# Hybrid decoder trunk on one core: zero products at the start, a reordered opening, and gate and keys of the second unit computed tile by tile with the first unit

## The chip, the cores and the metric

The kernel runs on one core of a Trainium2 chip. The metric is the device time of one execution in microseconds (us), lower is better; where several runs are compared, their median is used.

The engines are called by their names or by the short forms of the profile: TensorE (PE, its weight loads PEld), VectorE (DVE), ScalarE (ACT), GpSimd (POOL), and SyncE (SP), whose queue issues the kernel's DMAs.

## The reference, cut to what matters

One layer of a decoder trunk, 2048 tokens of width 1024, in float32:

```python
mod = (silu(c) @ w_ada + b_ada)                      # 6 x 1024: sh1, sc1, g1, sh2, sc2, g2
h = rms_norm(x) * (1.0 + sc1) + sh1
x = x + g1 * token_mixer(h, ...)                     # one input projection, three kinds of heads, one output projection
h = rms_norm(x) * (1.0 + sc2) + sh2
x = x + g2 * conv_ffn(h, ...)                        # up-projection, causal depthwise conv, silu gate, down-projection
return rms_norm(x) * final_gain
```

The token mixer has three groups of heads: HGRN2 heads (forget `f = lb + (1-lb)*sigmoid(z)`, key `1 - f` scaled by the bound, queries through silu, values, an output gate), GLA heads (a gate of rank 16: `logsigmoid(alow @ w_gla_up + b) / 16`, keys, queries, values, output gate) and retention heads (rotary, fixed decay). Each is a causal recurrence that is computed in chunks.

## The kernel before, in words

**Layout.** Tokens go in four blocks of 512 (`b`). Features lie on the partitions: the normalised input of a block is eight tiles `h[k]` of 128 features by 512 tokens. Every float32 product is made of three products of a split: each operand has a high part (rounded to the type that TensorE multiplies fast) and a low part (the rest), and `hi*hi + hi*lo + lo*hi` is accumulated (`split3`, lines 246 to 248). ScalarE casts the high part, VectorE subtracts to get the low part.

**Conditioning.** `mod` has 48 columns of 128. Column `m` is a dot product on VectorE of one weight tile (`wada[m]`, 512 KB) with `c_act = silu(c)`, which is held on all partitions (`ada`, line 197). Columns 0 to 7 are the shifts, 8 to 15 the scales of the first norm, one for each `h[k]`.

**Units.** The mixer of a block is a list of units: `ORDER = h0, g, h1, h2, h3, r0, r1`. `unit_h` makes the products for two HGRN2 heads (forget `f`, queries `q`, values and gates `vg`), `unit_g` those of the GLA heads (low-rank gate `al` and keys `ak`, then queries `aq`, then values and gates), `unit_r` those of retention. Behind its projections, each unit hands the recurrence to a chain (`gated`: dot products `dt`, seven levels `lv` of the chunk tree, transposes, state update, output, head norm `post`, transposed result `oT`). TensorE's order is the order of the program. A planner (`Clock`) decides where the chain's steps stand in it: each projection matmul that is emitted advances its clock (`adv`, 0.227 us for 512 columns), each chain step has a due time, and chains run one after another. `clock.until` empties due steps without products between them; one such place is ahead of the second half of the output projection of a block, in the next block behind its first unit. VectorE, ScalarE and SP are ordered by a scheduler with priorities (`tc.high_priority(offset)` puts instructions ahead by so many), except inside `startup`.

**The opening** (`startup`, lines 376 to 484) is the first block's norm together with the first unit's products, in an order written out by hand for VectorE, ScalarE and SP. The eight tiles of x are loaded, squared on ScalarE and summed on VectorE (line 346); four matmuls with a column of ones sum over partitions (`ssn`, line 418); a reciprocal square root is iterated on VectorE (`newton`); a matmul broadcasts it (`bcn`, line 426). Then for each tile k: `scaled` (line 352, VectorE), `high` (line 356, ScalarE), `low` (line 359, VectorE), and the products of the first unit that this tile allows, as far as the weights' parts are there (`put`, `flush`). The tuple `plan` says for each k which conditioning tiles are loaded, which dot products stand ahead of the scaling (`first`), which between high and low part (`then`), and which weight gets its low part. Weight tiles pass through two raw buffers (`wraw`), conditioning tiles through a ring of eight (`a4k`), on which SP waits in order.

**Around it.** `norm1_stat` and `norm1_h` make the norm of the next block during the current one; the broadcast follows the sums by 4.5 us of the planner's clock (`rstd`, line 330). `tok_evac` and `tok_evac4` read values and gates out of PSUM. The channel mixer behind the four blocks (from about 1,280 us on) is not touched.

Of the kernel before, what the change touches and what calls it, by code (L numbers as in the profile page):

```python
# [9 lines left out]
F32 = mybir.dt.float32  # L10
# [7 lines left out]
P = 128  # L18
# [29 lines left out]
CHAIN = 400  # L48

# [51 lines left out]
def trunk(ctx, tc, xT, vecs, cvec, cst, rope, msk, wada, win, walow, wgla, wout, wup, wdown, out):  # L101
# [39 lines left out]
    nc.sync.dma_start(vec[:], vecs)  # L141
# [7 lines left out]
    nc.sync.dma_start(c_all[:], cst)  # L149
# [13 lines left out]
    lg = vec[:, V_LB:V_LB + 4]  # L163
    e = small("lbe", 4)
    V.tensor_tensor(e[:], lg, lg, op=ALU.subtract)
    S.activation(e[:], e[:], AF.Exp)
    r = small("lbr", 4)
    V.reciprocal(r[:], e[:])
    V.tensor_tensor(e[:], e[:], r[:], op=ALU.mult)
    V.tensor_tensor(lb[:], e[:], e[:], op=ALU.subtract)  # L170
    V.tensor_scalar(oml[:], lb[:], -1.0, 1.0, op0=ALU.mult, op1=ALU.add)
# [4 lines left out]
    nc.sync.dma_start(craw[:], cvec.to_broadcast([P, D]))  # L176
    S.activation(c_act[:], craw[:], AF.Sigmoid)
    V.tensor_tensor(c_act[:], c_act[:], craw[:], op=ALU.mult)
# [3 lines left out]
    for g in (1, 4):  # L182
        V.tensor_scalar(bada1[:, 8 * g:8 * g + 8], bada1[:, 8 * g:8 * g + 8], 1.0, None, op0=ALU.add)

# [133 lines left out]
    def rstd(acc, name, bc, then, bank=None):  # L318
# [3 lines left out]
        def first():  # L322
# [7 lines left out]
            clock.at(4.5, lambda: second(r))  # L330
# [45 lines left out]
    def startup():  # L376
# [3 lines left out]
        for k in range(KD):  # L380
            x.append(x_tile(f"x0_{k}", k))
            nc.sync.dma_start(x[k], xT[0, :, k, :])
        raws = {}

        def weight(name, i, extra=False):
            raw = pw.tile([P, 1024], F32, tag="wraw", name="r" + name, bufs=NRAW)
            nc.sync.dma_start(raw[:], win[i])
            if extra:
                t = [pa.tile([P, 1024], F32R, tag="a4k", name=n + name) for n in "hl"]
            else:  # L390
                t = [pw.tile([P, 1024], F32R, tag="w" + n, name=n[0] + name) for n in ("hi", "lo")]
            W[name] = [*t, raw, i]

        def cast(name):
            S.copy(W[name][0][:], W[name][2][:])

        def low_part(name):
            hi, lo, raw, i = W[name]
            V.tensor_tensor(lo[:], raw[:], hi[:], op=ALU.subtract)

# [6 lines left out]
        load(8, 0)  # L407
        weight("f", 1)
        load(9)
        weight("q", 0)  # L410
        load(1, 2)
        acc = new_acc("n1_0")
        for k in range(KD):
            sumsq(acc, x[k], k, "n1_0_")
        cond(8)
        ps = late_ps("ssn1_0")
        for c in range(NCH):
            T.matmul(ps[:, c:c + 1], acc[:, c * P:(c + 1) * P], ones, start=True, stop=True)
        ms, r = small("msn1_0", NCH), small("rsn1_0", NCH)
        V.tensor_scalar(ms[:], ps[:, 0:NCH], 1.0 / D, EPS, op0=ALU.mult, op1=ALU.add)  # L420
        newton(ms, r, NCH)
        cast("f")
# [5 lines left out]
        cond(9)  # L428
        S.copy(bc[:], ps[:])
        cast("q")  # L430
# [3 lines left out]
        def put(kind, k, w):  # L434

            two = (0, 1) if w == 0 else (0,)
            if kind in "fq":
                sl = slice(k * P, (k + 1) * P)
                for p in two:
                    T.matmul((pf if kind == "f" else pq)[:], W[kind][w][:, sl], h[k][:, p, :],  # L440
                             start=k == 0 and w == 0 and p == 0, stop=k == KD - 1 and w == 1, skip_group_check=True)
            else:
                sl = slice((k % 4) * 256, (k % 4 + 1) * 256)
                for c in range(NCH):
                    for p in two:
                        T.matmul(pv[c // 2][:, (c % 2) * 256:(c % 2) * 256 + 256], h[k][:, p, c * P:(c + 1) * P],
                                 W[f"v{k // 4}"][w][:, sl], start=k == 0 and w == 0 and p == 0 and c % 2 == 0,
                                 stop=k == KD - 1 and w == 1 and c % 2 == 1, skip_group_check=True)

        def flush():  # L450
            for q in list(pending):
                if (q[0] if q[0] in "fq" else f"v{q[1] // 4}") in parts[q[2]]:
                    pending.remove(q)
                    put(*q)
# [4 lines left out]
        parts = {"f", "q"}, set()  # L459
        for k, (ld, first, then, wl) in enumerate(plan):  # L460
            if k == 0:
                weight("v0", 2)
            if k == 3:
                weight("v1", 3, True)
            load(*ld)
# [4 lines left out]
            if k in (1, 4):  # L470
                name = "v0" if k == 1 else "v1"
                cast(name)
                parts[0].add(name)
# [3 lines left out]
            if wl:  # L477
                low_part(wl)
                parts[1].add(wl)
            pending += [(kind, k, w) for w in (0, 1) for kind in "fqv"]  # L480
            flush()
        assert not pending
        ready["hfh0_0"], ready["hqh0_0"], ready["vgh0_0"] = pf, pq, pv
        return W

    def norm1_stat(b):
# [6 lines left out]
        clock.at(22.0, rstd(acc, f"n1_{b}", bc1[b][:], lambda: done.add(("n1", b))))  # L493
# [966 lines left out]
```

## Time and profile before

| | |
|---|---|
| median of 3 runs | 2587.08 us (2585.16 to 2595.53) |
| profiled execution | 2597.18 us, span 2595.4 us |
| TensorE busy | 2520.8 us, 97% of the span |
| VectorE busy | 1986.9 us, 77% |
| ScalarE busy | 1115.7 us, 43% |
| mean granted clock of TensorE | 0.992 |
| first product of the opening | 23.03 us |
| end of the opening's products | 58.42 us |

How to read it: the profile is of one execution, and its own time lies above the median of the runs. TensorE is nearly always busy, so time is to be had only where it waits or where its clock is lowered; the opening holds the longest such stretch. In the rows below, the first two numbers of a row of the timeline are start and duration in us, and the bracket at the end tells how long the engine had been idle and what ended that. A row that stands for several instructions gives their count behind an x.

### The profile page before, as it was taken

Reading aid. Unit: us, or ns where it says so; the run is one execution under the profiler, and the core shown is the slowest. Engines: PE = TensorE matmul, PEld = TensorE weight load, DVE = VectorE, ACT = ScalarE, POOL = GpSimd, SP = SyncE. Lnnn points to the kernel's source line nnn. Section 1 sums busy time; section 2 is a strip of 40 time slices with the busy share of each in tenths; the row PEclk is TensorE's granted clock in tenths of the full one; section 3 lists DMA queues with packets and bytes.
Section 4 is the critical chain, followed back from the end, with each engine's and each line's share of the span. In section 5 each row is a group of like instructions: output and inputs, shape, how many; then the busy total and the mean of one; then the engine's idle time right before and its main releaser. Section 6 shows DMA issues by size and latency. Waiting matters only on the chain.

```text
span 2595.4 us, 37081 instructions
## 1 busy us (share of the span) xinstructions
PE 2520.8 (97%) x13132; PEld 2137.3 (82%) x13132; DVE 1986.9 (77%) x3627; ACT 1115.7 (43%) x1897; POOL 144.2 (6%) x246
## 2 busy tenths in 40 slices
PE   5999999999999999999999999999999999999997
PEld 4798878998889888998778888878878888888886
DVE  8778986868768786887688888876677777788565
ACT  3333434433333234333355445455444544555442
POOL 1000010000000000000010000000000010010000
PEclk9999999999999999999999999999999999999998
DMA  8543656765687846877665444487665544447663
GB/s 304 192 156 131 213 215 232 276 211 181 220 294 273 291 166 221 298 278 254 221 221 170 151 154 147 157 277 237 204 224 165 158 136 146 150 134 271 200 189 111
DMA packets 231753, 533.88 MB, mean 206 GB/s; under 512 B 25072, under 2 KB 26128, under 8 KB 231568
## 3 DMA queue, kind: packets, MB, share of 16 engines
q1 hardware_dynamic: 231568, 531.52, 60.3%
q8 instruction: 103, 1.69, 0.3%
q14 instruction: 82, 0.67, 0.1%
HBM read 397.72 MB, written 133.69 MB: 205 GB/s over the span
## 4 chain that ended last, share of the span: by engine, by line
PE 88%; DVE 7%; DMA 3%; issue 1%; ACT 1%; SPq 0%; DVEq 0%; ACTq 0%
PE X L246 6%; PE X L247 6%; PE X L248 6%; PE lvh L622 3%; PE Z L247 3%; PE Z L248 3%; PE Z L246 3%; PE dX L246 3%; PE dX L248 3%; PE dX L247 3%; PE dY L246 2%; PE dY L248 2%; PE dY L247 2%; PE psqkvgr L248 2%; PE psqkvgr L246 2%; PE psqkvgr L247 2%
## 5 line engine op out<-in xcount | busy, mean ns | idle before, releaser
L246 PE MATMUL X<-B,A 128*128 128x512 f32 x572 | 224.5, 393 | 1.3 <-ACT u L1245 1.3
L247 PE MATMUL X<-B,A 128*128 128x512 f32 x572 | 223.9, 391 | 0.2 <-DMA B<-made 0.2
L248 PE MATMUL X<-B,A 128*128 128x512 f32 x572 | 223.9, 391 | 0.0
L973 DVE TENSOR_TENSOR dA<-rd,dA 128x512 fp32r<-128x512 f32 x154 | 106.3, 690 | 100.9 <-ACT dA L972 100.7
L972 ACT CAST dA<-rd 128x512 fp32r<-128x512 f32 x154 | 95.4, 619 | 159.5 <-PE dY L248 53.2
L973 DVE TENSOR_TENSOR A<-s,A 128x512 fp32r<-128x512 f32 x176 | 120.7, 687 | 40.9 <-ACT A L972 40.8
L246 PE MATMUL psvgh<-hvgh,ha 128*128 128x256 f32 x480 | 140.1, 292 | 0.0
L248 PE MATMUL dX<-dB,dA 128*128 128x512 f32 x352 | 139.1, 395 | 0.0
L247 PE MATMUL dX<-dB,dA 128*128 128x512 f32 x352 | 139.1, 395 | 0.0
L246 PE MATMUL dX<-dB,dA 128*128 128x512 f32 x352 | 139.1, 395 | 0.0
L248 PE MATMUL psvgh<-hvgh,ha 128*128 128x256 f32 x480 | 135.9, 283 | 0.0
L247 PE MATMUL psvgh<-lvgh,ha 128*128 128x256 f32 x480 | 135.9, 283 | 0.0
L972 ACT CAST A<-s 128x512 fp32r<-128x512 f32 x176 | 108.4, 617 | 61.8 <-PE Z L248 46.8
L246 PEld LDWEIGHTS X<-B,A 128*128 128x128 f32 x572 | 107.5, 188 | 25.1 <-ACT u L1245 2.2
L247 PEld LDWEIGHTS X<-B,A 128*128 128x128 f32 x572 | 107.5, 188 | 24.0 <-DMA B<-made 0.9
L248 PEld LDWEIGHTS X<-B,A 128*128 128x128 f32 x572 | 107.5, 188 | 23.2
L246 PE MATMUL Z<-B,A 128*128 128x512 f32 x308 | 122.0, 396 | 2.2 <-ACT B L972 1.7
L247 PE MATMUL Z<-B,A 128*128 128x512 f32 x308 | 121.7, 395 | 0.3 <-DVE B L973 0.3
L248 PE MATMUL Z<-B,A 128*128 128x512 f32 x308 | 121.7, 395 | 0.0
L622 PEld LDWEIGHTS lvh<-qbh,kh 128*128 128x128 f32 x896 | 115.2, 191 | 7.7 <-issue 1.4
L622 PE MATMUL lvh<-qbh,kh 128*128 128x128 f32 x896 | 120.1, 277 | 0.3 <-DVE kh L632 0.3
L973 DVE TENSOR_TENSOR A<-r,A 128x512 fp32r<-128x512 f32 x130 | 89.5, 688 | 30.3 <-ACT A L972 30.3
(440 smaller groups left out, 7127.7 us busy)
## 6 DMA issues: line engine op xcount, KB each, us to landing
gs<-yv SPq DMA_DIRECT2D x154, 256.0 KB, 2.8
rb<-gs SPq DMA_DIRECT2D x154, 256.0 KB, 4.0
r<-wup SPq DMA_DIRECT2D x141, 256.0 KB, 3.4
s<-sumsu SPq DMA_DIRECT2D x132, 256.0 KB, 3.0
wada<-wada SPq DMA_DIRECT2D x48, 512.0 KB, 4.8
rd<-sumsd SPq DMA_DIRECT2D x88, 256.0 KB, 3.8
rd<-wdown SPq DMA_DIRECT2D x66, 256.0 KB, 3.5
x<-xT SPq DMA_DIRECT2D x64, 256.0 KB, 5.1
```

What stands on the lines that cost most here:

```text
L246: T.matmul(ps, lhs[0], rhs[0], start=first, stop=False, skip_group_check=more)
L247: T.matmul(ps, lhs[0], rhs[1], start=False, stop=False, skip_group_check=more)
L248: T.matmul(ps, lhs[1], rhs[0], start=False, stop=last, skip_group_check=more)
L622: T.matmul(ps[:, c * P:(c + 1) * P].rearrange("p (h n s) -> p h n s", h=2, s=s), kq[:, c * P:(c + 1) * P], rhs, start=True, stop=True)
L972: S.copy(hi, src)
L973: V.tensor_tensor(lo, src, hi, op=ALU.subtract)
```

## The change

- **Zero products.** A tile of zeros is set on VectorE, and eight 128x512 float32 matmuls of it go ahead of all other products on TensorE, into a bank that is used later.
- **Opening, loads.** x comes in four DMAs of two tiles instead of eight of one; the vector c comes between the second and third of them, the constants (`cst`) behind the first conditioning tile. The gate's weights are loaded in the opening. Value weights go through other buffers, so that their load does not wait for a raw buffer.
- **Opening, conditioning.** The sigmoid of c stands behind the fifth square on ScalarE; the product for `c_act` and the additions to the bias stand behind the sums of squares on VectorE. Squares go to a ring of six buffers instead of two. In `plan`, the dot products stand ahead of the scaling for every tile but the first, and the first has two between high and low part (9 and 1).
- **Gate and keys of the GLA unit** (`l`: 16 matmuls, `k`: 24) are done in the opening tile by tile, in the two banks of the chain's levels. In block 0 `unit_g` takes them as ready, and the planner's clock is not advanced for them. `flush` emits products whose weights were there before the current tile ahead of those whose weights just came.
- **Read-out of values and gates** (`tok_evac`, `tok_evac4`) at a raised priority (`EVAC = 300`).
- **Forget factor and key of the HGRN2 units** on ScalarE instead of VectorE.
- **Broadcast of the next block's first norm** due 10.0 us of the planner's clock behind the sums, instead of 4.5.

```diff
@@ startup: head
+        still = tmp("still")
+        V.memset(still[:], 0.0)
+        nc.sync.dma_start(vec[:], vecs)
+        lower_bounds()
+        idle = acc_ps("idle")
+        for _ in range(8):
+            T.matmul(idle[:], still[:, 0:P], still[:], start=True, stop=True)
+        for k in range(0, KD, 2):
+            if k == 4:
+                nc.sync.dma_start(craw[:], cvec.to_broadcast([P, D]))
+            x += [x_tile(f"x0_{k}", k), x_tile(f"x0_{k}", k + 1)]
+            nc.sync.dma_start(pair[0][:].rearrange("p (a n) -> p a n", a=2), xT[0, :, k:k + 2, :])
...
+        acc = new_acc("n1_0")
+        S.activation(acc[:], x[0], AF.Square)
+        for k in range(1, KD):
+            t = tmp(f"sqn1_0_{k}")
+            S.activation(t[:], x[k], AF.Square)
+            V.tensor_tensor(acc[:], acc[:], t[:], op=ALU.add)
+            if k == 4:
+                S.activation(c_act[:], craw[:], AF.Sigmoid)
+        load(8)
+        nc.sync.dma_start(c_all[:], cst)
+        load(0)
         weight("f", 1)
+        al = gla_load()
         load(9)
         weight("q", 0)
-        load(1, 2)
+        load(1)
+        weight("v0", 2, "b")
+        load(10, 2)
+        V.tensor_tensor(c_act[:], c_act[:], craw[:], op=ALU.mult)
+        for g in (1, 4):
+            V.tensor_scalar(bada1[:, 8 * g:8 * g + 8], bada1[:, 8 * g:8 * g + 8], 1.0, None, op0=ALU.add)
@@ startup: order by tile (ld, first, then, wl)
-        plan = [((10,), (), (1,), "f"), ((3, 11), (), (2,), "q"), ((4,), (10,), (3,), "v0"),
-                ((12, 5), (11,), (4,), None), ((13, 6), (12,), (5,), "v1"), ((14, 7), (13,), (6,), None),
-                ((15,), (14,), (7,), None), ((), (15,), (), None)]
+        plan = [((11, 3, 12), (), (9, 1), "f"), ((4, 13), (), (), "q"), ((5,), (10, 2), (), "v0"),
+                ((14, 6), (11, 3), (), None), ((15, 7), (12, 4), (), "v1"), ((), (13, 5), (), "k"),
+                ((), (14, 6), (), None), ((), (15, 7), (), None)]
...
+            pending += [(kind, k, w, p) for w, p, kinds in ((0, 0, "fqvlk"), (0, 1, "fqvlk"), (1, 0, "fqvk"))
+                        for kind in kinds]
@@ tok_evac (tok_evac4 alike)
-            S.copy(v[:, c2, :], p3[:, :, 0:P])
-            S.activation(sg[:, c2, :], p3[:, :, P:256], AF.Sigmoid)
-            V.tensor_tensor(sg[:, c2, :], sg[:, c2, :], p3[:, :, P:256], op=ALU.mult)
+            with tc.high_priority(offset=EVAC):
+                S.copy(v[:, c2, :], p3[:, :, 0:P])
+                S.activation(sg[:, c2, :], p3[:, :, P:256], AF.Sigmoid)
+                V.tensor_tensor(sg[:, c2, :], sg[:, c2, :], p3[:, :, P:256], op=ALU.mult)
@@ unit_h
-        V.tensor_scalar(f[:], sf[:], oml[:, u:u + 1], lb[:, u:u + 1], op0=ALU.mult, op1=ALU.add)
-        V.tensor_scalar(kq[:], sn[:], oml[:, u:u + 1], None, op0=ALU.mult)
+        S.activation(f[:], sf[:], AF.Identity, bias=lb[:, u:u + 1], scale=oml[:, u:u + 1])
+        S.activation(kq[:], sn[:], AF.Copy, scale=oml[:, u:u + 1])
@@ norm1_stat, unit_g
-        clock.at(22.0, rstd(acc, f"n1_{b}", bc1[b][:], lambda: done.add(("n1", b))))
+        clock.at(22.0, rstd(acc, f"n1_{b}", bc1[b][:], lambda: done.add(("n1", b)), gap=10.0))
...
-        ps = acc_ps("al" + nm)
-        for k in range(KD):
+        ps = ready.pop("al" + nm, None) or acc_ps("al" + nm)
+        for k in range(KD if b else 0):
```

More of the change, by code (lines that the diff above doesn't have):

```diff
@@ L48 @@
 CHAIN = 400
+EVAC = 300
 M512, M256, MF = 0.227, 0.12, 0.224
@@ L315, in tf512, with rstd @@
         return pss
-    def rstd(acc, name, bc, then, bank=None):
+    def rstd(acc, name, bc, then, bank=None, gap=4.5):
         bank = bank or late_ps
@@ L329, in first @@
                 newton(x, r, NCH)
-            clock.at(4.5, lambda: second(r))
+            clock.at(gap, lambda: second(r))
         def second(r):
@@ L395, in cast @@
             S.copy(W[name][0][:], W[name][2][:])
+            parts[0].add(name)
         def low_part(name):
@@ L399, in low_part @@
             V.tensor_tensor(lo[:], raw[:], hi[:], op=ALU.subtract)
+            parts[1].add(name)
         def cond(m):
@@ L427, in startup, with put @@
         cond(0)
[L428 removed]
+        cast("f")
         S.copy(bc[:], ps[:])
[L430 removed]
         pf, pq = acc_ps("pshfh0_0"), acc_ps("pshqh0_0")
         pv = [acc_ps(f"psvgh0_0_{j}") for j in range(NCH // 2)]
[L434 to L437 removed]
+        pl, pk = lev_ps("alg0"), lev_ps("psakg0")
+        whole = {"f": pf, "q": pq, "k": pk}
+        def put(kind, k, w, p):
+            first, last = k == 0 and w == 0 and p == 0, k == KD - 1 and (w == 1 or kind == "l" and p == 1)
+            if kind == "l":
+                T.matmul(pl[0:32, :], alow[:, k, :], h[k][:, p, :], start=first, stop=last, skip_group_check=True)
+            elif kind in whole:
                 sl = slice(k * P, (k + 1) * P)
[L439 to L441 removed]
+                T.matmul(whole[kind][:], W[kind][w][:, sl], h[k][:, p, :], start=first, stop=last,
+                         skip_group_check=True)
             else:
@@ L469, in startup @@
             high(x[k], k, "0_")
[L470 to L473, printed above, removed]
+            for at, name in ((0, "q"), (1, "v0"), (3, "v1"), (4, "k")):
+                if k == at:
+                    cast(name)
             for m in then:
```

102 lines of the change are left out of this document (49 added, 53 removed).

## Prediction

> **What bounds the kernel now.** I read the page first, then busy time by stage, then the order of instructions of the first 71 us, then every wait of TensorE behind it.
>
> ```profile
> span 2595.4 us, 37081 instructions
> PE 2520.8 (97%) x13132; PEld 2137.3 (82%) x13132; DVE 1986.9 (77%) x3627; ACT 1115.7 (43%) x1897; POOL 144.2 (6%) x246
> PE 88%; DVE 7%; DMA 3%; issue 1%; ACT 1%; SPq 0%; DVEq 0%; ACTq 0%
> ```
>
> TensorE is busy for 2520.8 of 2595.4 us, so an edit that leaves its products alone can win at most the 74.6 us between, plus what a lowered clock costs. The profiled execution took 2597.2 us, its span and 1.8 around it; the median of the runs is 10.1 lower, so I sum against 2597.2 and take the difference off the median, 2587.1.
>
> ```profile
> 4.00:6.00 2.00, 0.00 (x0) 0.00 (x0) 0.69 (x2) 0.59 (x1) 1.89 (x5) 1.00 0.91 199
> 8.00:10.00 2.00, 0.00 (x0) 0.00 (x0) 1.77 (x3) 1.84 (x4) 1.31 (x3) 1.00 1.03 385
> 30.00:52.00 22.00, 18.97 (x104) 15.95 (x104) 21.58 (x33) 4.55 (x6) 2.87 (x3) 1.00 1.01 388
> 331.00:341.60 10.60, 10.60 (x40) 8.72 (x41) 7.53 (x17) 3.19 (x4) 3.12 (x5) 0.71 0.56 198
> 743.90:754.60 10.70, 10.62 (x42) 8.82 (x43) 5.62 (x12) 0.76 (x4) 0.00 (x0) 0.71 0.55 193
> ```
>
> Columns are PE, PEld, DVE, ACT, POOL, granted clock, DMA share, GB/s. From 30 to 52 us VectorE is busy for 21.58 of 22.00: the tile-by-tile opening is bound by VectorE, not by products. In the last two stretches the clock is 0.71; both follow a stall of TensorE (below). The lost 0.29 of 10.6 us is 3.1 us each.
>
> ```profile
> 3.31 1.28 ACT L177 ACT_TABLE_LOAD   x1
> 6.65 1.06 ACT L177 ACTIVATE c_act<-craw 128x1024 f32<-128x1024 f32 x1 [2.06 <-DMA craw<-cvec]
> 7.74 1.23 DVE L178 TENSOR_TENSOR c_act<-c_act,craw 128x1024 f32<-128x1024 f32 x1 [3.02 <-ACT c_act L177]
> 9.09 5.47 DVE L346 TENSOR_TENSOR san<-san,sqn 128x512 f32<-128x512 f32 x7
> 13.00 0.63 ACT L345 ACTIVATE sqn<-x 128x512 f32<-128x512 f32 x1 [0.16 <-DVE san L346]
> 16.52 0.16 DVE L420 TENSOR_SCALAR msn<-ssn 128x4 f32<-128x4 f32 x1 [0.75 <-PE ssn L418]
> 18.71 2.08 PE L426 MATMUL bcn<-c_all,rsn 128*128 128x128 f32 x8 [2.23 <-DVE rsn L158]
> 21.44 0.75 DVE L352 SCALAR_TENSOR_TENSOR x<-x,mod,bc 128x512 f32<-128x512 f32 x1 [0.38 <-ACT bc L429]
> 22.11 1.28 DVE L197 CUSTOM_DVE_ANT_0 wada<-wada,c_act,vec 128x1024 f32<-128x1024 f32 x1
> 23.31 0.75 DVE L359 SCALAR_TENSOR_TENSOR ha<-x,mod,ha 128x512 fp32r<-128x512 f32 x1
> 23.98 1.22 DVE L399 TENSOR_TENSOR lf<-rf,hf 128x1024 fp32r<-128x1024 f32 x1
> 25.11 0.75 DVE L352 SCALAR_TENSOR_TENSOR x<-x,mod,bc 128x512 f32<-128x512 f32 x1
> 30.15 1.28 DVE L197 CUSTOM_DVE_ANT_0 wada<-wada,c_act,vec 128x1024 f32<-128x1024 f32 x1 [1.08 <-DMA wada<-wada]
> 53.23 0.75 DVE L352 SCALAR_TENSOR_TENSOR x<-x,mod,bc 128x512 f32<-128x512 f32 x1
> 54.02 0.72 ACT L356 ACTIVATE ha<-x,mod 128x512 fp32r<-128x512 f32 x1 [3.14 <-DVE x L352]
> 54.78 0.75 DVE L359 SCALAR_TENSOR_TENSOR ha<-x,mod,ha 128x512 fp32r<-128x512 f32 x1 [0.79 <-ACT ha L356]
> 57.80 0.62 PE L446 MATMUL psvgh<-lv,ha 128*128 128x256 f32 x4
> 59.85 0.42 PE L743 MATMUL alg<-ha,alow 128*32 128x512 f32 x1 [1.42 <-ACT snh L707]
> 68.81 0.39 PE L248 MATMUL psakg<-ha,lakg 128*128 128x512 f32 x1
> 70.76 0.48 PE L246 MATMUL psaqg<-ha,haqg 128*128 128x512 f32 x1
> ```
>
> The sums of squares end at 14.56 (9.09 + 5.47). The first tile is scaled at 21.44, the last low half ends at 55.53, the products of the opening at 58.42. Gate and keys run from 59.85 to 69.04, and the gate unit's queries begin at 70.76, behind 1.7 us of the first unit's chain. From start to start VectorE spends 0.67 on a scaling or a low half, 1.20 on a conditioning dot product and 1.13 on a weight's low half.
>
> **The opening, step by step.** The gate (16 matmuls) and the keys (24) leave the stretch behind the opening: 59.85 to 69.04, 9.2 us, and the 1.43 us wait ahead of it. I take 69.0 as the time at which the old kernel would have begun the queries without that piece of chain, and ask when the new one does.
>
> *Sums of squares.* The x loads come in pairs with the vector c between the second and third. Two pairs of 0.52 MB at 385 GB/s take 2.7 us, c at the 199 GB/s of the stretch in which it was loading 2.6, the third pair 1.4; from 2.5 us, with 0.8 to landing, tile 4 is there at about 10.0 (8.5 to 11). ScalarE then runs in its fixed order: square 0.63, table load 1.28 and sigmoid 1.06, which now stand between square 4 and square 5, three squares at 0.66, and VectorE's last add 0.75: 15.7 against 14.56. The old kernel had that table load done while it waited for data. A reader of the Trainium skill, page "ScalarE: Activation LUTs", section "What ACT_TABLE_LOAD costs", finds about 2.66 us for a switch with its drain, and the advice to batch calls by set, which speaks against putting a sigmoid among the squares; the row shows 1.28, by the page the sum would be 1.4 us worse, and I keep the row.
>
> *To the first scaling.* The product for c_act (1.23) and the two small bias adds (some 0.4) now stand behind the sums, then one conditioning (1.28); the sums' matmuls are hidden under these. From there the old rows repeat: 16.52 to 18.71 for the square root, 18.71 to 21.44 for the broadcast. 15.7 + 1.2 + 0.4 + 1.3 + 2.2 + 2.7 = 23.5 against 21.44.
>
> *Scaling to last low half.* This took 34.1 us (21.44 to 55.53). Added: the conditioning of m = 9, which was ahead of it, 1.2; the keys' low half, 1.1. In the old plan a conditioning stood between scaling and low half of every tile but the last and covered ScalarE's high half; in the new one only tile 0 has that. The last tile's rows show the bare cost: 53.23 to 54.78 is 1.55 instead of 0.67, so 0.88 for each of six more tiles, 5.3. Gone: the wait of 1.08 at 30.15, since the value weights no longer queue on SP behind the forget weights' buffer. 34.1 + 1.2 + 1.1 + 5.3 - 1.1 = 40.6, so 64.1.
>
> *Tail and next stage.* Behind the last low half come 2.6 us of products against 2.9 before, so 67.0 with the same hand-over; the queries' first matmul then waits for a bank that ScalarE has to read out, and for its own weights' split, like the gate did: 1.4. That is 68.4 against 69.0: **a gain of 0.6 us**. Bounds: minus 3 (ScalarE reads out values before the forget bank) to plus 6 (tile 4 two us earlier, no table load, half of the six gaps filled). TensorE itself is no bound: the new products add five 128x512 matmuls a tile, 40 x 0.23 = 9.2 us, to a stretch in which VectorE needs 40.6.
>
> *Zero products.* They run while nothing else is there to do, so they cost nothing; only if cold and some 2 us each could they last to about 18 us, and c_act and conditioning cover that. Do they warm the clock for what follows? The 0.71 at 331 us stands behind waits of 2.63 and 1.57 us only (below). Between the zero products and the sums lie several us, and 4 us more before the broadcast, so I count no gain; if the clock held, the broadcast's 2.08 would halve, plus 1.0. The Trainium skill, "TensorE: Matmul & The Clock Gate", part 1, says that an idle window of about 3.4 us closes the gate again; by that rule the zero products warm nothing that the sum needs, and the trace agrees, with even shorter waits.
>
> **Behind the opening.**
>
> ```profile
> 114.08 0.50 PE L248 MATMUL pshfh<-ha,lhfh 128*128 128x512 f32 x1 [1.17 <-DVE lhfh L230]
> 132.27 1.12 PE L559 MATMUL oTh<-c_all,oh 128*128 128x128 f32 x4 [2.44 <-DVE oh L553]
> 328.93 0.50 PE L246 MATMUL pshfh<-ha,hhfh 128*128 128x512 f32 x1 [2.63 <-ACT ha L356]
> 330.99 0.79 PE L247 MATMUL pshfh<-ha,hhfh 128*128 128x512 f32 x1 [1.57 <-DVE ha L359]
> 399.42 0.79 PE L335 MATMUL bcn<-c_all,rsn 128*128 128x128 f32 x5 [0.89 <-DVE rsn L158]
> 743.98 0.76 PE L246 MATMUL pshfh<-ha,hhfh 128*128 128x512 f32 x1 [3.40 <-ACT sgg L539]
> L708 DVE TENSOR_SCALAR fh<-sfh,oml,lb x16: 539/546/566, 58.4 to 1128.0; 128x512 f32<-128x512 f32 x16
> L709 DVE TENSOR_SCALAR kh<-snh,oml x16: 480/486/765, 60.5 to 1128.5; 128x512 f32<-128x512 f32 x16
> L529 ACT COPY vh<-psvgh x32: 352/372/410, 60.2 to 1150.0; 128x256 f32<-128x256 f32 x32
>   PE psvgh L248: 46.9, 18
> ```
>
> *Raised priority of the read-out of values and gates.* At 743.98 TensorE waited 3.40 us for that read-out, and 3.1 of clock followed: 6.5. The new priority aims at it; I take 5 (0 to 6.5).
>
> *Forget and key on ScalarE.* 16 x (0.546 + 0.486) = 16.5 us leave VectorE for ScalarE, 43% busy. Waits that VectorE ends in blocks 0 and 1: 1.17 + 2.44 + 2.63 + 1.57 and 3.1 of clock, 10.9 (the 2.63 is ScalarE's by name, but its input is VectorE's scaling). With one instruction in some thirty gone I take a third, 3.5 (minus 4, if ScalarE's later forget factor holds up the decays, to 10.9).
>
> *Later broadcast of norm 1* (gap 10 for 4.5): 0.9, the 399.42 row.
>
> *The planner.* Its clock advances by 0.227 us for each 512-column matmul it emits. The 40 moved ones are no longer counted: 9.1 us of products fewer in block 0 beside chains of unchanged length, and the first chain starts after 9.0 us of queries and values instead of gate and keys. Adding up the planner's own constants, the chains of block 0 ended some 4 us ahead of where block 1 asks for them; now 3.4 us are missing, which TensorE waits out: minus 3.4 (minus 6.5 with a clock drop, to 0 if the real chain is ahead of plan).
>
> Sum: 0.6 + 5 + 3.5 + 0.9 - 3.4 = 6.6 us. 2597.2 - 6.6 = 2590.6 on the profile, **2580.5 us on the median**.
>
> **The rivals.** (1) *The opening works as meant*: the x data arrive two us earlier, ScalarE's high halves hide, the opening gains the 6 of its upper bound, and the later waits go as a whole: 6.5 + 10.9 + 0.9 instead of 9.4, minus 3.4: 20.9 us, 2566. For it: the waits are few, and all at places that the edits touch. Against: VectorE's fixed order, which the 1.55 us row shows.
> (2) *Slower: the raised read-out blocks ScalarE's queue.* ScalarE takes its instructions in order, and L529 already waits 46.9 us in 18 instances for values to be finished. If the read-out is put ahead of weight splits that were ready, the next products' weights come late. That decides once the added delay passes the slack of a weight, in more than half of the 28 read-outs: 28 x 0.8 us (one 0.37 copy and its sigmoid) is 22 us; with the 6.6 otherwise expected less the 5 that the read-out was to bring, 22 - 1.6: 2607.
> (3) *It doesn't do what it says*: opening as long as before, and for each wait that goes another comes: 2587.
>
> **How the numbers follow.** What a measurement of this kernel can tell from no change is about 0.5%, 13 us. Forecast 0.45, own range 2570 to 2592, of which 0.12 lies beyond 13 us of gain; rival 1 0.30, all faster; rival 2 0.20, all slower; rival 3 0.05. Faster 0.42, same 0.38, slower 0.20. The range runs from 2560 (the bounds of rival 1, less what is unlikely to come together) to 2606, and leaves out about 0.2: the far half of rival 2 and the tail of rival 1.
>
> **What would show it.** Right: the last sum of squares near 15.7 us with a table load among the squares; first scaling near 23.5; VectorE idle about 0.8 us before six more low halves, ended by ScalarE; last low half near 64; queries from about 68; clock at half behind the zero products; a wait for a transpose at the start of block 1; none for a read-out near 744. Wrong: the opening's products ending below 62 us, or TensorE waiting in many places for a weight's split behind a read-out.

## The result and the profile after

| | before | after |
|---|---|---|
| median of 12 runs each, side by side | 2594.2 us (2585.16 to 2600.97) | 2603.1 us (2598.73 to 2609.86) |
| ratio to before, 95% interval | | 1.0036 [1.0025, 1.0047] |
| profiled execution | 2597.18 us | 2601.29 us |
| first scaling; last low half; queries of the gate unit | 21.44; 54.78; 70.76 us | 24.20; 63.66; 68.67 us |
| dot products of the first chain (`dth`) | 69.04 us | 78.96 us |

The kernel became slower by 0.36%, some 9 us. That is inside the forecast's range and less than the 0.5% that the prediction took to be measurable, but the interval excludes no change and the sign is the other one: a gain of 6.6 us was forecast. The forecast's absolute times rest on the median of three runs of before, 2587.1; twelve runs gave 2594.2, so the comparison goes by the ratio. The two profiled executions differ by 4.1 us only, and each is a single draw; so sizes are taken from the ratios and the profile is read for places.

From the page of after:

```profile
span 2599.5 us, 37097 instructions
PE 2530.9 (97%) x13148; PEld 2140.8 (82%) x13148; DVE 1974.6 (76%) x3596; ACT 1134.9 (44%) x1929; POOL 144.4 (6%) x246
```

TensorE's busy time is 10.1 us more, of which the zero products are 9.56. They cover idle time and nothing else, so idle time on this page can't be compared with before as it stands.

From the timeline of after, the opening (start, duration, instruction, idle before and what ended it):

```profile
1.45 9.56 PE L383 MATMUL idle<-still 128*128 128x512 f32 x16 [1.45 <-DVE still L377]
11.64 1.28 ACT L426 ACT_TABLE_LOAD   x1
14.54 2.28 DVE L424 TENSOR_TENSOR san<-san,sqn 128x512 f32<-128x512 f32 x3 [2.20 <-ACT sqn L423]
24.20 0.75 DVE L348 SCALAR_TENSOR_TENSOR x<-x,mod,bc 128x512 f32<-128x512 f32 x1 [1.58 <-ACT bc L453]
46.94 0.75 DVE L355 SCALAR_TENSOR_TENSOR ha<-x,mod,ha 128x512 fp32r<-128x512 f32 x1 [0.79 <-ACT ha L352]
62.52 1.22 DVE L226 TENSOR_TENSOR laqg<-raqg,haqg 128x1024 fp32r<-128x1024 f32 x1
63.66 0.74 DVE L355 SCALAR_TENSOR_TENSOR ha<-x,mod,ha 128x512 fp32r<-128x512 f32 x1
68.67 0.50 PE L242 MATMUL psaqg<-ha,haqg 128*128 128x512 f32 x1 [1.04 <-DVE sgh L565]
72.92 0.69 DVE L750 TENSOR_TENSOR qkh<-sqh,kh 128x512 f32<-128x512 f32 x1
78.96 0.95 PE L646 MATMUL dth<-c_all,qkh 128*128 128x2 f32 x8
```

The opening went as it was worked out: the last sum ends at 16.82 (15.7 forecast, with the table load among the squares), the scaling starts at 24.20 (23.5), the last low half ends at 64.4 (64.1), the queries start at 68.67 (68.4). The table load took 1.28 us, and the sigmoid followed at once, at 12.94. The wait of 0.79 us behind the scaling stands in five tiles (46.94 is the fourth); in the last two it was filled, with a conditioning (57.58) and with the split of the query weight (62.52). What the prediction did not look at are the last two rows: the dot products' input is ready at 73.6, yet TensorE reaches them only at 78.96, with no wait, behind other products. In before the same product of queries and keys stands at 61.66 and the dots at 69.04: its chain starts 9.9 us earlier.

Time by stage, 55 to 480 us (columns as in the prediction), of before:

```profile
55.00:480.00 425.00, 410.04 (x2477) 358.32 (x2477) 335.43 (x744) 166.81 (x317) 17.98 (x29) 0.98 0.56 197
```

and of after, with two short stretches behind waits:

```profile
55.00:480.00 425.00, 404.08 (x2432) 354.48 (x2432) 332.63 (x731) 171.72 (x326) 23.75 (x39) 0.98 0.55 192
137.00:148.00 11.00, 10.55 (x66) 10.42 (x67) 7.89 (x12) 1.80 (x6) 0.00 (x0) 0.73 0.54 192
187.00:191.00 4.00, 4.00 (x16) 3.48 (x16) 2.69 (x5) 0.89 (x3) 1.04 (x2) 0.57 0.00 0
```

TensorE idles 20.9 us of these 425 in after against 15.0 in before. Where it idles, from the timeline of after:

```profile
137.45 1.12 PE L594 MATMUL oTh<-c_all,oh 128*128 128x128 f32 x4 [3.55 <-DVE oh L588]
184.66 0.85 PE L613 MATMUL og<-vg,atg 128*128 128x64 f32 x6 [1.29 <-DVE S L706]
287.47 0.72 DVE L588 TENSOR_TENSOR oh<-oh,sgh 128x512 f32<-128x512 f32 x1
288.23 0.79 ACT L574 ACTIVATE sgr<-psqkvgr 128x128 f32<-128x128 f32 x4 [2.56 <-DVE oh L588]
288.88 0.50 PE L242 MATMUL y<-oTh,hwo 128*128 128x512 f32 x1 [4.57 <-DVE sgr L575]
353.67 1.12 PE L646 MATMUL dth<-c_all,qkh 128*128 128x2 f32 x8 [1.84 <-DVE or L902]
366.86 0.63 PE L594 MATMUL oTr<-c_all,or 128*128 128x128 f32 x4 [2.65 <-DVE or L588]
750.49 0.47 PE L242 MATMUL pshfh<-ha,hhfh 128*128 128x512 f32 x1 [1.60 <-DVE sgg L575]
```

and the last transpose of block 0 in the timeline of before:

```profile
356.69 0.63 PE L559 MATMUL oTr<-c_all,or 128*128 128x128 f32 x4 [0.84 <-DVE or L553]
```

The five longest waits between 80 and 480 us are among these rows, and all five are for results of a chain, or for a buffer that a chain holds. The longest, 4.57 us, shows how: ScalarE could not read out the gates of a retention unit until VectorE's product of the output with an older gate (287.47) freed one of the three buffers of `sg`; until it did, the PSUM banks stayed full and the output projection could not start. Products had run ahead of the chains, and here they had to give the lead back. The wait for a transpose at the start of block 1 (366.86) was forecast at 3.4 us and came at 2.65; before already waits 0.84 us there (356.69). Of the other four, which were not forecast, that at 137 stands in before too, at 132.27 with 2.44 us; those at 184, 289 and 354 have no counterpart of 0.75 us or more in before. Before's waits near 329 us (2.63 and 1.57) are gone in after.

The loss is complete long before the end: the products ahead of the read-out wait that before has at 743.98 end at 740.6 us in before and at 748.9 in after (750.49 less the wait). The 8.3 us between them shrink to 4.1 by the end, near this place first: after waits 1.60 there, before 3.40 and then at a lowered clock.

### The profile page after: what moved, and what is told of

Same layout as the page of the kernel before. It is cut to its first block, busy times and chain, and to the rows that moved or that the text cites. A ratio compares the mean times of both kernels' runs of the same rounds, so it can differ in the third digit from the quotient of the medians.

```text
span 2599.5 us, 37097 instructions
## 1 busy us (share of the span) xinstructions
PE 2530.9 (97%) x13148; PEld 2140.8 (82%) x13148; DVE 1974.6 (76%) x3596; ACT 1134.9 (44%) x1929; POOL 144.4 (6%) x246
## 4 chain that ended last, share of the span: by engine, by line
PE 87%; DVE 7%; DMA 3%; ACT 1%; issue 1%; SPq 0%; DVEq 0%; ACTq 0%
PE X L242 6%; PE X L243 6%; PE X L244 6%; PE lvh L657 4%; PE Z L243 3%; PE Z L242 3%; PE Z L244 3%; PE dX L244 3%; PE dX L243 3%; PE dX L242 3%; PE y L242 2%; PE y L244 2%; PE dY L242 2%; PE dY L244 2%; PE dY L243 2%; PE y L243 2%
## 5 line engine op out<-in xcount | busy, mean ns | idle before, releaser
L242 PEld LDWEIGHTS X<-B,A 128*128 128x128 f32 x572 | 107.4, 188 | 25.8 <-ACT u L1282 2.2
```

Source lines behind the costliest of these rows:

```text
L242: T.matmul(ps, lhs[0], rhs[0], start=first, stop=False, skip_group_check=more)
```

## Experiments: the opening or the rest?

Each run below is compared with before on the same chip.

**opening_alone**: the kernel after without raised read-out, forget and key on ScalarE and later broadcast.

```diff
-            with tc.high_priority(offset=EVAC):
-                S.copy(v[:, c2, :], p3[:, :, 0:P])
...
-        S.activation(f[:], sf[:], AF.Identity, bias=lb[:, u:u + 1], scale=oml[:, u:u + 1])
+        V.tensor_scalar(f[:], sf[:], oml[:, u:u + 1], lb[:, u:u + 1], op0=ALU.mult, op1=ALU.add)
...
-        clock.at(22.0, rstd(acc, ..., gap=10.0))
+        clock.at(22.0, rstd(acc, ...))
```

> The new opening (zero products, loads, plan, gate and keys tile by tile, planner not advanced) with the old read-out priority, the old place of forget and key, and the old gap of 4.5. Theory 1 (the moved 9.2 us of gate and key products used to stand beside the start of block 0's first chain; the chains run one after another and now start 9.9 us later, 78.96 instead of 69.04, while the queries start no earlier, so the loss is the opening's): most or all of the slowdown is here, ratio to before 1.003 to 1.005 (+8 to +13 us), dots of the first unit near 79 us, last transpose of block 0 near 367 us instead of 357. Theory 2 (the raised read-out or the forget and key on ScalarE block a queue): ratio within 0.999 to 1.001, opening neutral as forecast.

**rest_alone**: the kernel before with just these three edits, `+` and `-` the other way round.

> The old opening with the raised read-out, forget and key on ScalarE and the gap of 10. Theory 1: no slower than before, ratio 0.996 to 1.000 (the waits at 329 and 744 us shrink), dots of the first unit near 69 us. Theory 2: it carries the slowdown, ratio 1.003 to 1.005.

Measured: opening_alone 1.0047 [1.0033, 1.006], 12.2 us slower; rest_alone 0.9987 [0.9977, 0.9997], 3.4 us faster. The two add up to 8.8 us of the 9.3 that the whole change costs. The loss lies in the opening edits, although the opening itself ended on time. Two expectations failed: the last transpose of block 0 came at 375.40 in opening_alone instead of near 367, and of the waits that rest_alone was to shorten, the one near 744 us fell to 1.60, while those near 329 us stayed (2.63 and 1.56). Where the loss shows is far behind it: the wait at the output projection, 4.57 us in after, is here the longest of the stage (timeline of opening_alone).

```profile
298.38 0.80 PE L242 MATMUL y<-oTh,hwo 128*128 128x512 f32 x1 [5.31 <-DVE sgr L573]
```

**readout_alone** and **forget_on_scalar** are the kernel before with one edit each:

```diff
@@ readout_alone, tok_evac (tok_evac4 alike)
+            with tc.high_priority(offset=EVAC):
@@ forget_on_scalar, unit_h
-        V.tensor_scalar(f[:], sf[:], oml[:, u:u + 1], lb[:, u:u + 1], op0=ALU.mult, op1=ALU.add)
-        V.tensor_scalar(kq[:], sn[:], oml[:, u:u + 1], None, op0=ALU.mult)
+        S.activation(f[:], sf[:], AF.Identity, bias=lb[:, u:u + 1], scale=oml[:, u:u + 1])
+        S.activation(kq[:], sn[:], AF.Copy, scale=oml[:, u:u + 1])
```

> The kernel before with the read-out of values and gates at raised priority, nothing else. My term was 5 us of gain (0 to 6.5), by the wait at 744 us and its lowered clock: ratio 0.998, no wait for a read-out near 744. If other waits take its place: 1.000. Rival 2 of the prediction (the read-out blocks ScalarE's queue): over 1.002.

> The kernel before with forget factor and key on ScalarE, nothing else. My term was 3.5 us of gain (minus 4 to 10.9): ratio 0.9985, waits at 132 and 329 us shorter. If VectorE's load is not what those waits hang on: 1.000, waits unchanged.

Measured: readout_alone 1.0003 [0.9994, 1.0013]; forget_on_scalar 0.9983 [0.9975, 0.9992]. From the timelines of readout_alone (first row) and of forget_on_scalar:

```profile
744.64 0.47 PE L247 MATMUL pshfh<-ha,hhfh 128*128 128x512 f32 x1 [2.37 <-DVE sgg L543]
```

```profile
130.47 0.66 PE L559 MATMUL oTh<-c_all,oh 128*128 128x128 f32 x4 [0.64 <-DVE oh L553]
325.00 0.49 PE L246 MATMUL pshfh<-ha,hhfh 128*128 128x512 f32 x1 [2.64 <-ACT ha L356]
327.07 0.80 PE L247 MATMUL pshfh<-ha,hhfh 128*128 128x512 f32 x1 [1.57 <-DVE ha L359]
737.30 0.47 PE L246 MATMUL pshfh<-ha,hhfh 128*128 128x512 f32 x1 [2.59 <-ACT sgg L539]
```

The raised read-out shortens the wait near 744 us from 3.40 to 2.37, not to nothing, and moving forget factor and key alone shortens it nearly as much, to 2.59. The waits near 329 us, which forget_on_scalar was to shorten, stayed as they were. The time by stage of readout_alone has a new slow stretch elsewhere; its rows, then before's for the first stretch:

```profile
114.00:130.00 16.00, 15.96 (x73) 14.78 (x74) 10.38 (x21) 3.65 (x8) 0.00 (x0) 0.68 0.32 115
743.90:754.60 10.70, 9.96 (x52) 8.59 (x53) 7.86 (x19) 2.84 (x7) 0.00 (x0) 1.00 0.79 272
```

```profile
114.00:130.00 16.00, 15.75 (x99) 13.78 (x99) 14.62 (x35) 4.67 (x10) 0.00 (x0) 1.00 0.57 197
```

In this execution the clock that was won at 744 us was lost again at 114. Rival 2 of the prediction (a raised read-out that blocks ScalarE's queue, 2607) lies near the measured time, but this run excludes it as the cause: 22 us of loss were priced, at most 3.4 fit the interval.

## Experiments: which part of the opening?

**plan_between**: after, with the conditioning of tiles 1 to 7 split again, one dot product ahead of the scaling, one between high and low part.

```diff
-        plan = [((11, 3, 12), (), (9, 1), "f"), ((4, 13), (), (), "q"), ((5,), (10, 2), (), "v0"),
+        plan = [((11, 3, 12), (), (9, 1), "f"), ((4, 13), (), (10,), "q"), ((5,), (2,), (11,), "v0"),
...
```

> The changed kernel, with one dot product of conditioning put back between scaling and low half in tiles 1 to 6 (and one ahead). If VectorE's waits for ScalarE's high half (0.79 us a tile) bind the opening: the first scaling stays at 24.2, the last low half ends 4 to 5 us earlier than 64.4, so do the queries (64 to 65 instead of 68.7) and the first unit's dots (74 to 75). Theory 1 then gives the whole kernel 3 to 5 us less than the changed one, ratio to before about 1.002. Theory 2: the queries come earlier but the total stays at 1.0036.

Measured: 1.0026 [1.0017, 1.0035]. The timeline of plan_between shows the queries 4.7 us earlier than in after:

```profile
64.00 0.50 PE L242 MATMUL psaqg<-ha,haqg 128*128 128x512 f32 x1 [1.04 <-DVE sgh L565]
```

The total is lower by 0.10%, 2.6 us, with intervals that overlap, so the run does not decide between its two theories. At the least, the 4.7 us did not come through whole: from 55 to 480 us TensorE idles 22.8 us here, against 20.9.

**chain_due_5**: after, with the first chain due 5.0 instead of 9.0 us behind the first unit.

```diff
-        clock.chain(gated(nm, b, u, pos, kq, decay, subs, qk, selh), 9.0 if b == u == 0 else 6.0)
+        clock.chain(gated(nm, b, u, pos, kq, decay, subs, qk, selh), 5.0 if b == u == 0 else 6.0)
```

> The changed kernel, with the first chain of block 0 due 5.0 us of the planner's clock behind its unit instead of 9.0, so that its first step stands ahead of the last queries. Theory 1 (late chains are the loss, not late products): dots at 75 us instead of 79, last transpose of block 0 some 4 us earlier, total 2 to 4 us less than the changed kernel (ratio to before 1.002), at the price of a wait of under 1 us for the unit's queries. Rival (the loss is PE waits that belong to the new order of products, not to the chain's start): no change, 1.0036.

Measured: 1.0025 [1.0014, 1.0035]. From the timeline of chain_due_5:

```profile
73.91 0.95 PE L646 MATMUL dth<-c_all,qkh 128*128 128x2 f32 x8
283.95 0.64 PE L242 MATMUL y<-oTh,hwo 128*128 128x512 f32 x1 [2.98 <-DVE sgr L575]
329.95 0.80 PE L242 MATMUL pshqh<-ha,hhqh 128*128 128x512 f32 x1 [4.30 <-ACT hhqh L222]
```

The dots come 5 us earlier, the waits for the `sg` ring and for the last transpose shrink (4.57 to 2.98, 2.65 to 0.35), but a wait of 4.30 for a weight's high part is new, and the idle time of the stage is 22.0 us. The total is 0.11%, 2.9 us, below that of after, with intervals that overlap. The edit moves the first chain by 4.0 of the 9.1 us that are no longer counted; whether that brings back its share, the run does not tell.

**keys_old_order** and **order_old_keys** part the opening in two: the first is before's opening in before's order, with gate and keys of the second unit added tile by tile (it keeps the buffers of the weights, the early load of the gate's weights and the `flush` of after); the second is the new order, loads and zero products, with gate and keys left in `unit_g`.

```diff
@@ keys_old_order, against before
-                ((12, 5), (11,), (4,), None), ((13, 6), (12,), (5,), "v1"), ((14, 7), (13,), (6,), None),
+                ((12, 5), (11,), (4,), None), ((13, 6), (12,), (5,), "v1"), ((14, 7), (13,), (6,), "k"),
...
-        for k in range(KD):
+        for k in range(KD if b else 0):
@@ order_old_keys, against opening_alone
-            pending += [(kind, k, w, p) for w, p, kinds in ((0, 0, "fqvlk"), (0, 1, "fqvlk"), (1, 0, "fqvk"))
+            pending += [(kind, k, w, p) for w, p, kinds in ((0, 0, "fqv"), (0, 1, "fqv"), (1, 0, "fqv"))
...
-        for k in range(KD if b else 0):
+        for k in range(KD):
```

> The kernel before, with only gate and keys of the second unit done tile by tile in the opening (value and key weights in other buffers, planner not advanced); loads, sums and conditioning in the old order, no zero products, old read-out, old place of forget and key, gap 4.5. It tells the moved products from the new order. Theory 1 (block 0 is paced by its chains, which start when the first unit's products and their conditioning on VectorE are done): opening's products end at 60 to 61 us, queries near 62 to 63 (6 us earlier than without the change), but dots near 72 (3 us later); ratio to before 1.000 to 1.0015. Rival (products pace the block; the loss of opening_alone is only the late opening): 6 us faster, ratio 0.9975 to 0.999.

> The counterpart: the new opening (zero products, paired loads, sigmoid among the squares, conditioning ahead of the scaling) but gate and keys left in the second unit as before, planner as before; old read-out, forget and key, gap. Theory 1: opening's products end near 65 us instead of 58.4, dots near 76 instead of 69, queries as late; products and chains both 6 to 7 us late: ratio to before 1.002 to 1.003, so more than half of opening_alone's 1.0047. Rival (the moved products are the whole loss): 1.000 to 1.001.

Measured: keys_old_order 1.0030 [1.0019, 1.0041], 7.8 us; order_old_keys 1.0017 [1.0006, 1.0028], 4.4 us. They add up to opening_alone's 12.2, with some 3 us of uncertainty on each. For keys_old_order neither theory gave so much, 1.0015 at most. Order_old_keys lies between its theory and its rival, and it holds the zero products as well as the new order. From the timeline of keys_old_order:

```profile
62.81 1.38 DVE L742 TENSOR_TENSOR qbh<-sqh,fh 64x512 f32<-64x512 f32 x2
71.76 0.39 PE L634 MATMUL dth<-c_all,qkh 128*128 128x2 f32 x3
287.85 0.79 PE L242 MATMUL y<-oTh,hwo 128*128 128x512 f32 x1 [5.31 <-DVE sgr L563]
367.38 0.63 PE L582 MATMUL oTr<-c_all,or 128*128 128x128 f32 x4 [2.50 <-DVE or L576]
```

Here the queries begin at 60.51, 10.2 us earlier than in before, and the kernel is slower all the same. The inputs of the chain are complete at 64.2, the dots stand at 71.76: the program puts them there, for the planner places a chain's steps by the products it has counted, and the 40 of gate and keys are no longer counted. By the planner's rule, then, each step of a chain stands behind 9.1 us more of the later products than before, as long as the chains follow each other without a pause.

**one_zero_product**: after, with one call of the zero product instead of eight.

```diff
-        for _ in range(8):
+        for _ in range(1):
             T.matmul(idle[:], still[:, 0:P], still[:], start=True, stop=True)
```

> The kernel after with one pair of zero products instead of eight pairs before the first real product. By the prediction they carry no gain, since the clock is at half speed in the first real products anyway: ratio 1.003 to 1.004, as the kernel after, clock at half until about 34 us in both. Rival (the products keep the clock up for part of the opening): 2 to 4 us slower than the kernel after, 1.0045 to 1.005, and a later end of the half-speed stretch.

Measured: 1.0019 [1.001, 1.0028], below the 1.003 to 1.004 expected: not slower than after, so the zero products bring nothing that can be measured. Whether they cost something is open; the intervals overlap by a hair, and the two timelines name no cost (first scaling 24.08 against 24.20, dots 78.57 against 78.96). So the 0.17% of order_old_keys may be the new order's or the zero products'.

## Experiments: the planner's count

**after_counted**: after, with the planner's clock moved on, where the second unit starts, by the products that it no longer sees.

```diff
+        if not b:
+            clock.t += 40 * M512
         ps = ready.pop("al" + nm, None) or acc_ps("al" + nm)
```

> The kernel after, but where the second unit starts, the emitting planner's clock is moved on by the 40 products (9.1 us) of gate and keys that it no longer sees there, so the first chain is put in 9.1 us earlier among the later products, beside the same neighbours as before the change. Main theory (the loss is an order of work in which products run ahead of the chains and give the lead back with interest): dots of h0 at about 70 us instead of 78.96, the last transpose of block 0 at about 357 instead of 366.86, TensorE's waits from 55 to 480 us together about 15 instead of 20.9; ratio to before 0.998 to 1.001, against 1.0036. Rival (the loss is the later start of the opening itself, S at 24.2 instead of 21.4 and the idle between low halves): nothing moves, 1.0025 to 1.0045.

Measured: **0.9986 [0.9977, 0.9994]**. These two lines, which issue no instruction, take the changed kernel from 1.0036 to 0.9986: 13 us, give or take 4, and from slower to faster than before. Its time by stage and its timeline:

```profile
55.00:480.00 425.00, 410.46 (x2500) 361.87 (x2499) 337.58 (x749) 176.35 (x334) 23.72 (x39) 0.98 0.60 201
```

```profile
73.70 1.87 PE L646 MATMUL dth<-c_all,qkh 128*128 128x2 f32 x8 [4.04 <-DVE qkh L750]
77.35 2.05 PE L657 MATMUL lvh<-qbh,kh 128*128 128x128 f32 x8 [1.77 <-DVE qbh L754]
135.23 0.73 PE L594 MATMUL oTh<-c_all,oh 128*128 128x128 f32 x4 [3.05 <-DVE eh L630]
354.55 0.60 PE L594 MATMUL oTr<-c_all,or 128*128 128x128 f32 x4
738.84 0.47 PE L242 MATMUL pshfh<-ha,hhfh 128*128 128x512 f32 x1 [1.60 <-DVE sgg L575]
```

TensorE now stands still for the dots and the first level, 4.04 and 1.77 us, which looks like a loss in the opening, and the waits at 184, 289, 354 and 367 us are gone: 14.5 us idle from 55 to 480 against 20.9. The dots come at 73.70, not at the 70 expected, since their input is ready no earlier. The wait of after at 137.45 stays, with 3.05 us, and the last transpose of block 0 comes at 354.55 with no wait. Of the 9.8 us between the two spans, these idle times are 6.4; the rest lies in no one place that could be named. But it too is gained early: the products ahead of the read-out wait, which end at 748.9 us in after, end at 737.2 here.

**keys_counted**: the same two lines in keys_old_order.

> The kernel before with gate and keys of the second unit tile by tile beside the first (keys_old_order, which measured 1.0030 [1.0019, 1.0041]), and the planner's clock moved on by their 9.1 us where the second unit starts. Main theory: the dots are put in as soon as their inputs are ready (about 64 to 66 us instead of 71.76), the last transpose of block 0 near 353 to 356 instead of 367.38, the waits from 55 to 480 us fall from 25.0 to about 15 to 18; ratio 0.997 to 1.000. Rival (the keys cost by what they need early: their weights on VectorE and their psum banks): the waits move but the ratio stays at 1.002 to 1.004.

Measured: 0.9994 [0.9984, 1.0004], from 1.0030. The idle time from 55 to 480 falls from 25.3 to 19.3 us; the second row is from the time by stage of keys_counted, the first from that of keys_old_order.

```profile
55.00:480.00 425.00, 399.72 (x2413) 350.52 (x2412) 330.54 (x732) 162.87 (x314) 22.52 (x37) 0.98 0.56 191
```

```profile
55.00:480.00 425.00, 405.69 (x2448) 355.73 (x2448) 335.95 (x742) 165.24 (x317) 22.46 (x37) 0.98 0.57 196
```

Both openings, old order and new, lose by the missing count and recover with it. The rival, that the keys cost by what they need early, fails: the keys in the opening cost 0.30% without the count, and nothing that can be measured with it. The idle time fell less than expected, to 19.3 us instead of 15 to 18.

**keys_counted_rest**: keys_counted with forget and key on ScalarE and the later broadcast.

```diff
-        V.tensor_scalar(f[:], sf[:], oml[:, u:u + 1], lb[:, u:u + 1], op0=ALU.mult, op1=ALU.add)
+        S.activation(f[:], sf[:], AF.Identity, bias=lb[:, u:u + 1], scale=oml[:, u:u + 1])
...
-        clock.at(22.0, rstd(acc, ...))
+        clock.at(22.0, rstd(acc, ..., gap=10.0))
```

> keys_counted with forget gates and keys on ScalarE and the later broadcast as well. Main theory: the two gains add, 0.9983 of forget_on_scalar on top of keys_counted's: ratio 0.994 to 0.9985, TensorE's wait near 744 us gone. Rival (in block 0 the same slack serves both, so only one of them counts): 0.9975 to 0.9995.

Measured: **0.9952 [0.9939, 0.9965]** in five runs, median 2582.3 us, 12.5 us faster than before by the ratio and the best of all kernels here. From its time by stage and its timeline:

```profile
55.00:480.00 425.00, 412.62 (x2573) 365.92 (x2572) 339.78 (x763) 176.92 (x337) 24.75 (x42) 0.99 0.61 204
```

```profile
64.45 1.84 PE L634 MATMUL dth<-c_all,qkh 128*128 128x2 f32 x8 [3.92 <-DVE qkh L738]
728.96 0.47 PE L242 MATMUL pshfh<-ha,hhfh 128*128 128x512 f32 x1 [4.29 <-ACT sgg L562]
```

12.4 us idle from 55 to 480, less than any other. The gain is more than the sum of keys_counted (0.06%) and forget_on_scalar (0.17%); why they help each other was not taken apart. One part of the expectation failed: the wait that stood near 744 us is not gone, it stands at 728.96 with 4.29 us. Against after_counted this kernel has the old order of the opening, no zero products and no raised read-out, and is another 0.34% faster. The raised read-out moved nothing by itself. New order and zero products together cost 0.17% (order_old_keys), half of that, and the new opening puts the queries at 68.7 instead of 59.6 us. Which of them the 0.34% belong to is open: neither was run by itself with the count restored.

## Why the prediction was wrong, step by step

- **The planner, minus 3.4 (minus 6.5 to 0): the step that failed.** The mechanism was named, but it was priced at one place, the `until` at the start of block 1. Even there the starting point was off. The chains of block 0 were taken to be 4 us ahead, yet the trace of before already waits 0.84 us for that transpose, and the wait grew by 1.8 us, to 2.65. And from 4 us ahead to 3.4 missing are 7.4 us, though 9.1 us of products left the count. Above all, the count sets the place of every step of every chain in block 0, not of the last one only. The trace of after has new waits for chains at 184, 289 and 354 us (7.7 us together), a longer one at 137, and slow stretches behind them. Restoring the count is worth 13 us (9 to 17) in the changed kernel: nearly four times the value taken, and twice the bound. In keys_old_order it is worth 9 us.
- **The opening, gain 0.6: its milestones held, in part by luck.** Each came within 1.2 us. No run shows the 0.8 us to landing that the first of them uses; the square of tile 4 started at 11.00, when its DMA released it, instead of 10.0. Six more gaps of 0.88 us were summed. Five came, and the old one in the last tile went, so four more are left, 1.8 us less than summed. The split of the query weight (1.22 us at 62.52) was not in the sum and makes up for most of that. As for the gain, the whole change with the count restored gains 3.6 us (0.9986) and the rest alone 3.4. That leaves 0.2 for the opening, give or take 3, if the gains add, which they do not in keys_counted_rest. What the step didn't see is that the new opening eats what the moved products bring: before's order with the same products has its queries at 60.5.
- **Zero products, no gain: held** (one_zero_product). That they cost nothing is not shown.
- **Raised read-out, 5 (0 to 6.5): mis-sized.** Measured minus 0.8 (minus 3.4 to plus 1.6). The wait shrank by 1.0 us and the clock there recovered, but half-speed time came back elsewhere; that a local gain of clock stays was assumed, not argued.
- **Forget and key on ScalarE, 3.5: the size held, 4.4 (2.1 to 6.5), the reason only in part.** Of the waits summed, the one at 132.27 shrank from 2.44 to 0.64 us; the 1.17 at 114 and the 2.63 and 1.57 near 329 us did not move. The wait near 744 us, which was not in this term, shrank too. "One instruction in some thirty" is off as well: 32 of the some 2,180 that VectorE runs from 55 to 1,280 us are one in 68. That the third came out right is luck.
- **Later broadcast, 0.9**: not run by itself. All three late edits together gave 3.4 where 9.4 was summed, nearly the whole difference being the read-out's.
- **The chances.** Rival 2 was the only case priced as slower; the case that came about was in the sum as a small term with one place, so it got no chance of its own. A term whose mechanism acts at many places needed that rival: all chains of a block late by the 9.1 us that are no longer counted.

The signs of the opening that the prediction named as showing it right did show, with five gaps of 0.8 us for six. The wait for a transpose at the start of block 1 came too. The wait for a read-out near 744 us, of which none was to be left, was still there, 1.60 us at 750.49. The sign that would have told more, the start of the first chain, was not on the list.

## What to carry to other kernels

Where a program's order is planned by counting work, moving work out of the count moves everything that is placed by it: look for what reads the counter before you price the move. Judge a shortened stage by the first thing that the next stage waits for, not by its own end: here a stage that handed over 10 us earlier made the kernel slower. A wait that stands early, in the open, can be cheaper than the lead that avoids it, since a lead over serial chains is given back at ring buffers and deadlines: here 5.8 us of waits for the first chain went with a kernel that was 13 us faster.

## What the runs showed of the hardware

**A granted clock of 1.00 ahead of the first busy stretch is no measurement.** The time by stage from 14 to 34 us reads 0.51 in after and 1.00 in one_zero_product:

```profile
14.00:34.00 20.00, 10.62 (x31) 7.50 (x32) 16.53 (x35) 6.70 (x10) 0.00 (x0) 0.51 0.88 340
```

```profile
14.00:34.00 20.00, 10.74 (x31) 7.59 (x32) 16.66 (x35) 6.57 (x10) 0.00 (x0) 1.00 0.87 338
```

Busy times are the same, and so are the products: a 128x512 product takes 0.79 to 0.80 us at 25.8 us in after and 0.80 at 25.64 in one_zero_product, and 0.40 from about 34 and 35 us on. TensorE ran at half speed there in both, as in before (0.79 at 23.03, 0.40 at 34.62). The zero products did get TensorE to full speed: their weight loads start 0.85 us apart at first (5.03, 5.88) and 0.43 from 6.55 on (6.55, 6.99, 7.42). But they ended at 11.01, and the speed was lost again ahead of the first real products: the clock of after is 0.87 from 11 to 14 us and 0.50 from 14 to 17. What they added is that this fall is on record. The prediction quoted such rows of 1.00 for 4 to 10 us; they say nothing of the clock.

**Slow stretches stand behind short waits too.** A wait of 1.29 us at 184.66, followed by small products (128x64), stands ahead of a clock of 0.57 from 187 to 191 us, and the wait of 3.55 us at 137.45 goes with 0.73 from 137 to 148. The Trainium skill, "TensorE: Matmul & The Clock Gate", part 1, has the clock fall behind an idle window of about 3.4 us and calls the windows free-running; the first of these waits is far shorter, so by that rule the small products would have to count as nearly idle, which no run here tells apart.
